# Fourteen late gate groups of a hybrid linear-attention block: plain products replaced by Strassen block products over pairs of groups and pairs of token tiles

## The chip, the cores and the metric

The kernel runs on one core of one Trainium2 chip. The metric is the device time of one execution in microseconds (us). Engines are called as the profile calls them: PE (TensorE matmul), PEld (its weight loads), DVE (VectorE), ACT (ScalarE), POOL (GpSimd) and SP (SyncE, which issues the DMAs here).

## The reference, cut to what matters

One adaLN-modulated layer over 2048 latent tokens with a context prefix of 256 tokens, model width 1024, all in float32. A modulated RMSNorm gives `h`; one wide projection of `h` feeds everything else, among it the output gates of two linear-attention mixers (GLA and Gated DeltaNet) and the 2048 columns of merge gates:

```
z = jnp.matmul(h, w_in).astype(f32)
aq, ak, av, ag, alr, bq, bk, bv, bg, bbeta, bdec, mg = split_cols(z)
...
gates = jax.nn.sigmoid(mg + b_gate.astype(jnp.float32))
merged = gates[..., :D_MODEL] * jnp.matmul(ya, w_gla_out) + gates[..., D_MODEL:] * jnp.matmul(yb, w_gdn_out)
return jnp.matmul(merged, w_o)
```

The change touches only how a part of `mg` (14 of its 16 groups of 128 columns) is computed from `h` and `w_in`.

## The kernel before, in words

The work is four stages one behind the other: a front (modulation vector, RMSNorm, transposes), a projection stage, the chunk-wise preparation of Gated DeltaNet ("gdn"), and then the scans ("mix") and the output stage. PE runs its instructions in the order in which they stand in its queue, and so do DVE, ACT, POOL and SP; a scheduler of the tile framework writes these five queues when the kernel is built, from the order of the program, from its own model of readiness, and from when buffers come free.

**The operands.** `h` is kept in SBUF transposed and split in two: `hi` (the value rounded to the matmul's fp32r format) and `lo` (the rest). The latent tokens are four tiles of 512, each tile with 8 slices of 128 rows of `h` (KD = 8). A weight group of 128 columns of `w_in` is loaded raw (512 KB, `raw_w`), split by ACT into `wh` and by POOL into `wl` (`split_w`). A product of one group with one tile (`tile_mm`, L371) is 8 x 3 = 24 matmuls of 128x128 by 128x512: hi by hi, hi by lo, lo by hi, summed in one PSUM buffer `pz` of three. `gate_eat` (L420) then makes the tanh on ACT and SP writes the tile to `d_gate` in DRAM.

**Where the gates stand.** Groups 8 and 9 are made in the front, groups 0 to 7 in the projection stage (`slots`, one group after the other over all four tiles), and the other fourteen, 10 to 23, are the *late* groups: `gates_dense` is a generator over 14 groups x 4 tiles x 4 steps of 6 matmuls = 224 steps. `phase_proj` weaves it with the gdn preparation: 18 chunks of 128 tokens and one step more, each with its share `int(total * (i + 1) / (NCH + 1.25))` of the steps, so 224/19.25 = 11.6 steps to a chunk.

**The gdn preparation.** `gdn_front(c)` makes the masks and key products of chunk c: POOL multiplies the log-decays by a mask (`R`, L914, four a chunk), PE sums them (L920, L921), ACT takes the exp (L923), POOL multiplies (`n`, L917 and L924; `dec`, L926), PE forms the key products (L936), DVE multiplies them in (L940), ACT and POOL split `n` into `nhi` and `nlo` (L945, L946). `gdn_solve(d, c)` inverts a triangular matrix for both directions by doubling: PE (L988), ACT (L989), PE (L995, L996), DVE (L873), six times over, then POOL's `rt` (L1001), DVE (L1006), and three more products. Front of chunk c and solve of chunk c-1 stand in the same weave.

## Time and profile before

| | us |
|---|---|
| median of 3 runs (lowest, highest) | 2163.72 (2163.07, 2163.72) |
| profiled execution, time | 2161.12 |
| its span, first to last instruction | 2159.3 |
| busy: PE, DVE, ACT, POOL | 2062.3, 1215.5, 899.0, 858.6 |
| last tanh of an early gate, start | 828.86 |
| last tanh of a late gate, start | 1362.9 |

A "row" of the page or of a view has the source line, the engine, the operation, output and input tiles, shapes, the count after an x, then busy time and the mean duration of one in ns; behind the second bar stands how long the engine sat idle just before these instructions, and what ended the wait. The window rows give, for a stretch of the execution, its length, the busy time of each engine with the number of instructions, the granted PE clock (1.00 is full), the share of the DMA engines and GB/s. A matmul's duration is longer than its spacing to the next, since matmuls are pipelined: the pace is read from start to start.

### The profile page before, as it was taken

What the parts mean: (1) busy time and instruction counts of PE and PEld (TensorE: products, weight loads), DVE (VectorE), ACT (ScalarE), POOL (GpSimd) and SP (SyncE); (2) the same over time, 40 slices, a digit from 0 to 9 for tenths busy, and PEclk for the clock granted to TensorE, in tenths of its full rate; (3) what the DMA queues carried; (4) which work ended last, traced back from release to release, by engine and by line L of the source; (5) the groups of instructions that cost most, each with busy time, mean ns of one, the idle gap of its engine ahead of it and who ended that gap; (6) DMA issues with size and microseconds to landing.
All of it is one profiled execution on the core that took longest, in us unless ns stands there. A gap on an engine that the chain in (4) does not pass through costs nothing.

```text
span 2159.3 us, 41811 instructions
## 1 busy us (share of the span) xinstructions
PE 2062.3 (96%) x16096; PEld 1730.3 (80%) x16096; DVE 1215.5 (56%) x2185; ACT 899.0 (42%) x2212; POOL 858.6 (40%) x779
## 2 busy tenths in 40 slices
PE   5999999999999999999999999899988888999998
PEld 2688888888888888777777777788888777999888
DVE  3813555556777553556555555566677776444333
ACT  4644255555452223443434443355555554112111
POOL 2410122222221015666666663456566664222331
PEclk9999999999999999999999999999999999999999
DMA  8323122222222224444434344778888868333222
GB/s 288 104 86 116 50 69 64 63 62 72 61 62 80 71 80 133 138 138 152 143 127 148 128 142 140 262 286 292 308 281 288 285 212 273 130 134 114 98 88 79
DMA packets 275012, 315.60 MB, mean 146 GB/s; under 512 B 22280, under 2 KB 206844, under 8 KB 274812
## 3 DMA queue, kind: packets, MB, share of 16 engines
q1 hardware_dynamic: 274812, 312.92, 43.9%
q8 instruction: 127, 2.08, 0.4%
q14 instruction: 73, 0.60, 0.1%
HBM read 203.00 MB, written 109.84 MB: 145 GB/s over the span
## 4 chain that ended last, share of the span: by engine, by line
PE 82%; DVE 5%; ACT 5%; DMA 3%; POOL 2%; issue 2%; SPq 1%; DVEq 0%; POOLq 0%; ACTq 0%
PE pz L371 46%; PE pz L1661 8%; PE pm L1592 8%; DMA g<-dg 2%; PE pe L936 1%; PE pe L1118 1%; PE pl L995 1%; PE pl L988 1%; PE pl L996 1%; PE pz L1080 1%; DVE ql L1215 1%; ACT E L1209 1%; PE pz L1059 1%; PE pq L614 1%; PE pz L1347 1%
## 5 line engine op out<-in xcount | busy, mean ns | idle before, releaser
L371 PE MATMUL pz<-hi,wh 128*128 128x512 f32 (+1 forms) x1560 | 621.6, 399 | 1.5 <-DVE hi L134 1.5
L371 PE MATMUL pz<-lo,wh 128*128 128x512 f32 (+1 forms) x1560 | 600.3, 385 | 1.8 <-POOL lo L135 1.8
L371 PE MATMUL pz<-hi,wl 128*128 128x512 f32 (+1 forms) x1520 | 588.4, 387 | 0.0
L371 PEld LDWEIGHTS pz<-lo,wh 128*128 128x128 f32 x1560 | 294.7, 189 | 51.0 <-POOL lo L135 3.6
L371 PEld LDWEIGHTS pz<-hi,wh 128*128 128x128 f32 x1560 | 294.3, 189 | 47.8 <-DVE hi L134 2.4
L371 PEld LDWEIGHTS pz<-hi,wl 128*128 128x128 f32 x1520 | 286.1, 188 | 53.9 <-issue 0.4
L135 POOL TENSOR_TENSOR wl<-w,wh 128x1024 fp32r<-128x1024 f32 x44 | 110.0, 2500 | 437.5 <-ACT wh L132 312.0
L569 DVE SCALAR_TENSOR_TENSOR acc<-zpad,cw,acc 128x1024 f32<-128x1024 f32 x192 | 272.3, 1418 | 6.6
L1592 PE MATMUL pm<-yh,wab 128*128 128x256 f32 x1024 | 188.2, 285 | 2.2 <-ACT fsq L1402 1.4
L873 DVE CAST_PREDICATED U<-kit,pl 128x256 f16<-128x256 int32 x216 | 91.1, 431 | 139.2 <-PE pl L996 135.4
L1592 PEld LDWEIGHTS pm<-yh,wab 128*128 128x128 f32 x1024 | 161.8, 193 | 3.1 <-ACT fsq L1402 1.6
L1661 PE MATMUL pz<-wo,mh 128*128 128x512 f32 (+1 forms) x528 | 161.3, 388 | 0.0
L1592 PE MATMUL pm<-yl,wab 128*128 128x256 f32 x512 | 145.5, 284 | 0.0
L989 ACT CAST ppb<-pl 128x256 f16<-128x256 f32 x216 | 73.5, 373 | 166.7 <-PE pl L988 160.3
L1216 POOL TENSOR_TENSOR E<-E,ak 128x256 f32<-128x256 f32 x96 | 78.9, 841 | 110.6 <-ACT E L1209 67.0
L1661 PEld LDWEIGHTS pz<-wo,mh 128*128 128x128 f32 x528 | 98.2, 189 | 20.1
L135 DVE TENSOR_TENSOR sql<-sq,sqh 128x512 fp32r<-128x512 f32 (+1 forms) x36 | 28.0, 804 | 140.5 <-ACT sqh L132 140.2
L624 POOL TENSOR_TENSOR acc<-acc,sq 128x512 f32<-128x512 f32 x32 | 50.6, 1586 | 137.7 <-ACT sq L623 77.7
L1661 PE MATMUL pz<-wo,ml 128*128 128x512 f32 (+1 forms) x264 | 102.0, 386 | 0.0
L1592 PEld LDWEIGHTS pm<-yl,wab 128*128 128x128 f32 x512 | 98.9, 193 | 0.3
L135 POOL TENSOR_TENSOR yl<-wr,yh 128x1024 fp32r<-128x1024 f32 x16 | 39.2, 2462 | 128.2 <-ACT yh L132 128.2
L1666 DVE TENSOR_TENSOR mt<-pz,gtb 128x512 f32<-128x512 f32 (+1 forms) x33 | 22.3, 675 | 115.3 <-PE pz L1661 113.1
(299 smaller groups left out, 4117.5 us busy)
## 6 DMA issues: line engine op xcount, KB each, us to landing
dgate<-ob SPq DMA_DIRECT2D x96, 256.0 KB, 2.1
gd<-dgd SPq DMA_DIRECT2D x32, 768.0 KB, 7.5
w<-in_w_in SPq DMA_DIRECT2D x44, 512.0 KB, 3.6
qk<-dqkv SPq DMA_DIRECT2D x32, 512.0 KB, 6.0
ga<-dgate SPq DMA_DIRECT2D x64, 256.0 KB, 2.8
dqkv<-acc SPq DMA_DIRECT2D x192, 64.0 KB, 1.6
dgd<-tm SPq DMA_DIRECT2D x36, 256.0 KB, 2.9
dgd<-n SPq DMA_DIRECT2D x36, 256.0 KB, 3.4
```

Source lines behind the costliest of these rows:

```text
L135: getattr(nc, lo).tensor_tensor(dst_lo, src, dst_hi.bitcast(F32), op=ALU.subtract)
L371: nc.tensor.matmul(ps[:, 0:n], a[:, kk, :], b[:, kk, :], start=(k == 0), stop=(k == last - 1))
L569: nc.vector.scalar_tensor_tensor(acc, src, wcol, acc, op0=ALU.mult, op1=ALU.add)
L614: nc.tensor.matmul(u[4][:, 0:u[2]], self.ones, u[3][i], start=(i == 0), stop=(i == 1))
L624: nc.gpsimd.tensor_tensor(v, v, r, op=ALU.mult)
L873: self.nc.vector.copy_predicated(out, mv, data)
L936: nc.tensor.matmul(ps[:, o + a * P:o + 256], qk[:, 1, h, :], kq[:, h, a:2, :], start=True, stop=True)
L989: nc.scalar.copy(ppl, pc.rearrange("p h (j i) -> p h j i", i=m))
L1216: nc.gpsimd.tensor_tensor(E[:, :, li, 1], E[:, :, li, 1], k, op=ALU.mult)
L1592: nc.tensor.matmul(ps[:, half * 256:half * 256 + 256], wab[wi][:, k, j * P:(j + 1) * P], yy[:, k, :], start=(i == 0), stop=(i == 11))
L1661: nc.tensor.matmul(ps, aa[:, k, i * P:(i + 1) * P], wo[k][wi][:, cs], start=(j == 0), stop=(j == 23))
L1666: nc.vector.tensor_tensor(sq, ps, gtb[:, cs], op=ALU.mult)
```

## The change

The late groups are taken two by two (7 pairs), and the token tiles two by two (0 with 1, 2 with 3), 14 units in all. In a unit the two weight groups, cut in two halves of the 1024 rows, are a 2x2 block matrix A, and the two token tiles, cut the same way, a 2x2 block matrix B. Winograd's form of Strassen's product needs seven block products instead of eight:

- sums of weights: S1 = A21+A22, S2 = S1-A11, S3 = A22-S2, S4 = A12-S2, made by DVE (`w_sums`) for every unit, and the hi/lo split of the seven left factors (`w_halves`: ACT, and POOL for five, DVE for two);
- sums of tokens: T1 = B12-B11, T3 = B22-B12, T2 = T1-form plus B22, T4 = B21-T2, made once for each pair of tiles, split again into hi and lo, and put in place of tiles that are no longer needed. For that the front writes every slice of `h` to DRAM (`d_h`, 32 DMAs of 256 KB), and `h_first`, `h_fourth` and `h_next` read it back;
- each product is 4 x 3 = 12 matmuls (L558 of the changed kernel, "DENSE" for short below); seven products are 84 matmuls where the plain form had 96. The fourteen units are 1176 matmuls instead of 1344, in 196 steps of 6 instead of 224;
- three PSUM buffers a unit (`a`, `c`, `b`) are summed over several products; between them ACT copies intermediate sums to SBUF (four a unit), DVE adds two, POOL one, and ACT makes the same four tanh as before.

The pair (0, 1) needs T1, T2, T3, T4 when the late gates begin: `h_first` and `h_fourth` hang on the last early gate group, whose tiles are taken in the order 2, 3, 1, 0; T1 to T3 are built in place of tiles 2 and 3 behind its second tile, T4 behind its third. The pair (2, 3) is built during the seventh unit (`h_next`). The weights of the first pair are loaded into a pool that lies where the buffers of `h_first` lay. Pools `wz` and `zs` move to the other side of SBUF.

```diff
+PRODUCTS = (("A11", "B11"), ("S1", "T1"), ("S2", "T2"), ("A12", "B21"), ("S3", "T3"), ("S4", "B22"), ("A22", "T4"))
...
         x2ctx = ExitStack()
         hx2 = self.pool("hx2", 4, ctx=x2ctx)
         hc = self.pool("hTc", 1, ctx=actx, side="right")
+        self.wz = self.pool("wz", 2, ctx=actx, side="right")
+        self.zs = self.pool("zs", 2, ctx=actx, side="right")
         tiles = [(2 + 4 * i, 4, 0) for i in range(4)] + [(0, 2, 1)]
         self.hT = [None] * 5
 
...
+            b, ks = k2 // 2, slice(2 * (k2 % 2), 2 * (k2 % 2) + 2)
+            self.split(hi[b][:, ks, ws], lo[b][:, ks, ws], ht, hi="vector", lo="vector" if k2 % 2 else "gpsimd")
+            if ti < 4:
+                nc.sync.dma_start(self.d_h[ti][b][:, ks, ws], ht)
             yield
...
-                nc.tensor.matmul(ps[:, 0:n], a[:, kk, :], b[:, kk, :], start=(k == 0), stop=(k == last - 1))
+                nc.tensor.matmul(ps[:, 0:n], a[:, kk, :], b[kk // 4][:, kk % 4, :], start=(k == 0), stop=(k == last - 1))
...
-    def gates_dense(self, groups, w):
...
-                yield from self.tile_mm(w, self.hT[ti], self.gate_eat(g), 6)
-                if ti == 1 and raw is not None:
-                    nw = self.split_w(raw)
+    def halves(self, hi, lo, raw, eng):
+        self.nc.scalar.copy(hi, raw.bitcast(F32))
+        eng.tensor_tensor(lo, raw.bitcast(F32), hi.bitcast(F32), op=ALU.subtract)
+
+    def h_raw(self, dst, i, k):
+        self.nc.sync.dma_start(dst.bitcast(F32), self.d_h[i][k])
+
+    def h_sum(self, dst, a, b, op):
+        self.nc.vector.tensor_tensor(dst, a.bitcast(F32), b.bitcast(F32), op=op)
+
+    def h_split(self, blk):
+        self.halves(*blk, blk[1], self.nc.gpsimd)
...
+    def h_t123(self, pieces, t1, t2, t3):
+        for k in range(KD // 2):
+            b11, b12, b22, x, y = pieces(k)
+            self.h_sum(y, b22, b12, ALU.subtract)
+            self.h_sum(x, b12, b11, ALU.subtract)
+            self.halves(t1[0][:, k], t1[1][:, k], x, self.nc.gpsimd)
+            self.halves(t3[0][:, k], t3[1][:, k], y, self.nc.vector)
+            self.h_sum(y, y, b11, ALU.add)
+            self.halves(t2[0][:, k], t2[1][:, k], y, self.nc.gpsimd)
+
+    def h_t4(self, t4, t2, i):
+        for k in range(KD // 2):
+            x = self.hr.tile([P, 512], F32, name=f"r{k % 2}")
+            self.nc.sync.dma_start(x, self.d_h[i][1][:, k])
+            self.h_sum(x, x, t2[0][:, k], ALU.subtract)
+            self.h_sum(x, x, t2[1][:, k], ALU.subtract)
+            self.halves(t4[0][:, k], t4[1][:, k], x, (self.nc.gpsimd, self.nc.vector)[k % 2])
+
+    def h_first(self):
+        b = self.hb8 = [(self.hT[i][2][k], self.hT[i][3][k]) for i in range(4) for k in range(2)]
+        self.hctx.close()
+        self.hr = self.pool("hr", 2, ctx=self.hctx)
+
+        def pieces(k):
+            r = [self.hr.tile([P, 512], F32, name=f"r{j}") for j in range(3)]
+            for t, (i, h) in zip(r, ((0, 0), (1, 0), (1, 1))):
+                self.nc.sync.dma_start(t, self.d_h[i][h][:, k])
+            return *r, r[1], r[2]
+        self.h_t123(pieces, b[4], b[6], b[5])
+
+    def h_fourth(self):
+        b = self.hb8
+        self.h_t4(b[2], b[6], 0)
+        self.hb = {"B11": b[0], "B21": b[1], "T2": b[6], "T1": b[4], "T3": b[5], "B22": b[3], "T4": b[2]}
+
+    def h_next(self, p, i):
+        o = [self.hb[r] for _, r in PRODUCTS]
+        if p == 0:
+            self.h_raw(o[0][1], i, 0)
+            self.h_raw(o[0][0], i + 1, 0)
+        elif p == 1:
+            self.h_raw(o[1][1], i + 1, 1)
+        elif p == 4:
+            raws = o[0][1], o[0][0], o[1][1]
+            self.h_t123(lambda k: (*[t[:, k] for t in raws], *[self.hr.tile([P, 512], F32, name=f"r{j}") for j in range(2)]),
+                        o[2], o[4], o[3])
...
+        elif p == 5:
+            self.h_raw(o[5][1], i, 1)
+            self.h_split(o[5])
+        elif p == 6:
+            self.h_split(o[1])
+            self.h_t4(o[6], o[4], i)
+            self.hb = {"B11": o[0], "B22": o[1], "T1": o[2], "T3": o[3], "T2": o[4], "B21": o[5], "T4": o[6]}
+
+    def w_raws(self, pair):
+        wv = self.io["w_in"].rearrange("o (k p) n -> p (o k) n", p=P)
+        w = {}
+        for i, g in enumerate(pair):
...
+            for j in range(2):
+                nm = f"A{i + 1}{j + 1}"
...
+
+    def w_sum(self, w, nm, a, b, op):
+        w[nm] = self.ws.tile([P, KD // 2, P], F32, name="r0" if nm in ("S1", "S3") else "r1", bufs=1) if nm != "S4" else w[b]
+        self.nc.vector.tensor_tensor(w[nm], w[a], w[b], op=op)
...
+    def w_sums(self, w, part):
+        if part == 0:
+            self.w_sum(w, "S1", "A21", "A22", ALU.add)
+            self.w_sum(w, "S2", "S1", "A11", ALU.subtract)
+        else:
+            self.w_sum(w, "S3", "A22", "S2", ALU.subtract)
+            self.w_sum(w, "S4", "A12", "S2", ALU.subtract)
+
+    def w_halves(self, w, p):
+        nm = PRODUCTS[p][0]
+        tile_ = lambda n, b: self.ws.tile([P, KD // 2, P], F32R, name=n, bufs=b)
+        hi, lo, raw = tile_("hi", 4), tile_("lo", 4), w[nm]
+        self.halves(hi, lo, raw, self.nc.vector if nm in ("S1", "S4") else self.nc.gpsimd)
+        w[p] = (hi, lo)
...
+    def gate_fin(self, ob, src, g, ti):
+        nc = self.nc
+        nc.scalar.activation(ob, src, AF.Tanh, bias=self.pc[:, 48 + g - 8:49 + g - 8], scale=0.5)
+        b0 = 2 * ti
...
+
+    def gates_dense(self, pairs):
+        nc = self.nc
+        work = [(pr, ti) for ti in (0, 2) for pr in pairs]
+        tile_ = lambda: self.zs.tile([P, 512], F32, name="ob")
+        w = self.w_raws(pairs[0])
+        self.w_sums(w, 0)
...
+        self.w_sums(w, 1)
+        for i, ((g0, g1), ti) in enumerate(work):
+            nw = self.w_raws(work[i + 1][0]) if i + 1 < len(work) else None
+            for p, (_, r) in enumerate(PRODUCTS):
+                if p == 0:
+                    a = ps = self.pv()
+                elif p == 1:
...
+                    b = ps = self.pv()
...
+                k = 0
...
+                    for x, y in ((0, 0), (0, 1), (1, 0)):
+                        nc.tensor.matmul(ps, w[p][x][:, kk, :], self.hb[r][y][:, kk, :],
+                                         start=(k == 0 and p in (0, 1, 3)), stop=(k == 11), skip_group_check=True)
+                        k += 1
+                        if k == 6:
+                            yield
+                if p in (0, 1, 2, 4):
+                    s = tile_()
+                    nc.scalar.copy(s, ps)
+                if p == 0:
...
+                    s5 = s
+                elif p == 2:
...
+                elif p == 5:
+                    nc.vector.tensor_tensor(s2, c, s2, op=ALU.add)
+                    self.gate_fin(s2, s2, g0, ti + 1)
+                else:
+                    s = tile_()
+                    self.gate_fin(s, a, g1, ti)
+                if p < 4:
+                    self.w_halves(w, p + 3)
+                elif nw is not None:
+                    self.w_halves(nw, p - 4)
+                if nw is not None and p in (3, 6):
+                    self.w_sums(nw, 0 if p == 3 else 1)
...
-    def slots(self, slots, raw, after, w=None):
+    def slots(self, slots, raw, after, w=None, last=None):
...
+            if last and i + 1 == len(slots):
+                tiles = [self.hT[j] for j in last]
...
+            self.d_h = [[dp.tile([P, KD // 2, 512], F32, name=f"dh{i}_{k}") for k in range(2)] for i in range(4)]
...
-            w = self.slots(seq, None, self.gate_cols(late[0]), w)
+            hooks = seq[-1][3]
+            hooks.setdefault(1, []).append(self.h_first)
+            hooks.setdefault(2, []).append(self.h_fourth)
+            self.slots(seq, None, None, w, last=(2, 3, 1, 0))
...
+            self.hctx.close()
+            self.ws = self.pool("ws", 2, ctx=ctx)
+            self.zs = self.pool("zs2", 4, ctx=ctx)
...
-            dense = self.gates_dense(late, w)
-            total = len(late) * 4 * 4
+            pairs = list(zip(late[0::2], late[1::2]))
+            dense = self.gates_dense(pairs)
+            total = len(pairs) * 2 * 14
```

Three places show how the queues move. **PE, where the late gates begin**, before. L371 are the matmuls of a group with a tile (here the first late group, which follows the last early one without a break), L920 and L921 the sums of log-decays of gdn:

```order
L371 MATMUL pz<-hi_214,wl 128x512
L371 MATMUL pz<-hi_214,wh 128x512
L371 MATMUL pz<-lo_215,wh 128x512
L371 MATMUL pz<-hi_214,wl 128x512
L920 MATMUL pe<-R,m_6471 128x512
L921 MATMUL pe<-R,m_6471 128x512
L371 MATMUL pz<-hi_214,wh 128x512
L371 MATMUL pz<-lo_215,wh 128x512
L371 MATMUL pz<-hi_214,wl 128x512
```

The same place in the changed kernel, where L375 are the last matmuls of the last early group, L1091 and L1092 stand for L920 and L921, L1107, L1123 and L1131 are the key products of the gdn front (L936, L952 and L960 before) and L1150 a transposition that uses `nhi` (L979 before):

```order
L375 MATMUL pz<-hi_1_223,wh 128x512
L375 MATMUL pz<-lo_1_225,wh 128x512
L375 MATMUL pz<-hi_1_223,wl 128x512
L1091 MATMUL pe<-R,m_6612 128x512
L1092 MATMUL pe<-R,m_6612 128x512
L1091 MATMUL pe<-R,m_6612 128x512
L1092 MATMUL pe<-R,m_6612 128x512
L1107 MATMUL pe<-gqk 128x128 x4
L1123 MATMUL pe<-kf,gqk 128x128 x4
L1131 MATMUL pe<-kf,gv 128x128 x4
L1150 LDWEIGHTS nhi
L1150 MATMUL pl<-id_6613,nhi 128x64
```

Where late matmuls stood, gdn work of the first chunk now follows, and the first late matmul (L558) comes 29 rows below the last one shown, behind the first solve steps (L1159, L988 before).

**POOL at the same place**, before. L914, L917 and L924 are the products of the gdn front, `wl` is the weight split, `nlo` the split of `n`:

```order
L914 TENSOR_TENSOR R<-ghi,kf 128x512
L914 TENSOR_TENSOR R<-glo,kf 128x512
L917 TENSOR_TENSOR n_6509<-negb,kf 128x512
L917 TENSOR_TENSOR n_6533<-negb,kf 128x512
L917 TENSOR_TENSOR n_6677<-negb,kf 128x512
L135 TENSOR_TENSOR wl<-w,wh 128x1024
L914 TENSOR_TENSOR R<-ghi,kf 128x512
L914 TENSOR_TENSOR R<-glo,kf 128x512
L924 TENSOR_TENSOR n_6509<-n_6509,dec 128x512
L914 TENSOR_TENSOR R<-ghi,kf 128x512
L914 TENSOR_TENSOR R<-glo,kf 128x512
```

In the changed kernel `lo_...<-r_...` are splits of token sums (T1 to T4 of the first pair of tiles), `lo<-A...` and `lo<-r...` with plain `hi` splits of left factors (A11 and S2), L1085, L1088, L1095 and L1117 the former L914, L917, L924 and L946:

```order
L432 TENSOR_TENSOR lo_0_232<-r_6492,hi_0_230 128x512
L432 TENSOR_TENSOR lo_0_918<-r_6493,hi_0_916 128x512
L432 TENSOR_TENSOR lo_0_228<-r_6535,hi_0_226 128x512
L432 TENSOR_TENSOR lo_0_228<-r_6547,hi_0_226 128x512
L1117 TENSOR_TENSOR nlo<-n_6644,nhi 128x512
L1117 TENSOR_TENSOR nlo<-n_6710,nhi 128x512
L1088 TENSOR_TENSOR n_6944<-negb,kf 128x512
L1085 TENSOR_TENSOR R<-ghi,kf 128x512
L1085 TENSOR_TENSOR R<-glo,kf 128x512
L432 TENSOR_TENSOR lo<-A_6646,hi 128x512
L1095 TENSOR_TENSOR n_6867<-n_6867,dec 128x512
L432 TENSOR_TENSOR lo<-r_6656,hi 128x512
```

A11's split, which the first block product reads, is the tenth of these rows. From the first split of a token sum to this row POOL has 27 rows, eleven of them splits of 128x512; before, one `wl` of 128x1024 stood among the same products of gdn.

**POOL where the seventh unit hands over to the eighth**, in the changed kernel: the last splits of T1 and T2 of the second pair of tiles (`r_...`), of B22, B11 and B21 (128x2048), of a left factor, and between them the former L914 to L926, L946 and L1001 (L1085 to L1097, L1117, L1172):

```order
L1097 TENSOR_TENSOR dec<-dec,kf 128x512
L1073 TENSOR_TENSOR R<-R 128x256
L432 TENSOR_TENSOR lo_0_918<-r_10778,hi_0_916 128x512
L432 TENSOR_TENSOR lo_1_233<-r_10768,hi_1_231 128x512
L432 TENSOR_TENSOR lo<-r_10663,hi 128x512
L432 TENSOR_TENSOR lo_0_232<-lo_0_232,hi_0_230 128x2048
L432 TENSOR_TENSOR lo_0_224<-lo_0_224,hi_0_222 128x2048
L432 TENSOR_TENSOR lo_1_229<-lo_1_229,hi_1_227 128x2048
L432 TENSOR_TENSOR lo_1_233<-r_10779,hi_1_231 128x512
L1117 TENSOR_TENSOR nlo<-n_10703,nhi 128x512
L432 TENSOR_TENSOR lo<-A_10309,hi 128x512
L1172 TENSOR_TENSOR rt<-id_6613,U 128x512 x2
```

In a chunk of the kernel before, the same stretch of the gdn work holds one late split:

```order
L924 TENSOR_TENSOR n_7166<-n_7166,dec 128x512
L926 TENSOR_TENSOR dec<-dec,kf 128x512
L914 TENSOR_TENSOR R<-ghi,kf 128x512
L924 TENSOR_TENSOR n_7237<-n_7237,dec 128x512
L926 TENSOR_TENSOR dec<-dec,kf 128x512
L902 TENSOR_TENSOR R<-R 128x256
L946 TENSOR_TENSOR nlo<-n_7166,nhi 128x512
L1001 TENSOR_TENSOR rt<-id_6472,U 128x512 x2
L946 TENSOR_TENSOR nlo<-n_7237,nhi 128x512
L135 TENSOR_TENSOR wl<-w,wh 128x1024
L917 TENSOR_TENSOR n_7611<-negb,kf 128x512
```

Three splits of 128x2048 and the splits of the token sums stand ahead of that chunk's `nlo` and `rt`, where one `wl` of 128x1024 stood.

51 lines of the change are left out of this document (36 added, 15 removed).

## Prediction

> **What bounds the kernel now.** I read the page first, then the windows over the stretch in which the late gates are made, then the chain of waits inside that stretch. The page's chain by engine, and its first lines by source line:
>
> ```profile
> PE 82%; DVE 5%; ACT 5%; DMA 3%; POOL 2%; issue 2%; SPq 1%; DVEq 0%; POOLq 0%; ACTq 0%
> PE pz L371 46%; PE pz L1661 8%; PE pm L1592 8%; DMA g<-dg 2%; PE pe L936 1%; PE pe L1118 1%; PE pl L995 1%; PE pl L988 1%; PE pl L996 1%; PE pz L1080 1%; DVE ql L1215 1%; ACT E L1209 1%; PE pz L1059 1%; PE pq L614 1%; PE pz L1347 1%
> ```
>
> Nearly half of the span is L371, of which the late gates are a part. The windows (length, then busy time of PE, PEld, DVE, ACT and POOL, then granted clock, DMA share, GB/s), first over the start of the late gates and then over the body of the stage:
>
> ```profile
> 815.00:830.00 15.00, 15.00 (x68) 12.43 (x67) 7.27 (x13) 3.28 (x5) 7.46 (x8) 1.00 0.48 150
> 830.00:845.00 15.00, 15.00 (x75) 12.50 (x74) 4.54 (x9) 4.93 (x8) 11.63 (x10) 1.00 0.48 143
> 830.00:1330.00 500.00, 497.17 (x4901) 386.84 (x4900) 281.54 (x727) 205.03 (x458) 312.58 (x270) 1.00 0.42 137
> ```
>
> PE is busy 497.17 of 500 us; POOL, 312.58, comes second. The stage (828.86 to 1362.9 in the table above, 534 us) is PE's, and at its start PE has no gap at all. So every matmul taken out here shortens the kernel by its spacing, and every stretch in which PE finds no matmul ready lengthens it by its full length. The change does both.
>
> **What it removes.** Pieces of the chain, in order of time (start, length, what):
>
> ```profile
> 1086.20 1.46 PE pz L371 x6
> ...
> 1089.86 0.31 PE pe L920
> 1090.17 0.24 PE pe L921
> ...
> 1092.39 0.86 PE pe L936 x4
> 1093.25 0.23 PE pl L988 x8
> 1093.48 1.45 PE pz L371 x6
> ...
> 1098.16 0.44 PE pe L952 x4
> ...
> 1101.42 0.45 PE pe L960 x4
> ```
>
> A step of six late matmuls costs 1.46 us on the chain. It was 224 steps and becomes 196: 28 x 1.46 = **-41 us**. Between two tiles of the last early group, which nothing interrupts, the spacing is
>
> ```profile
> 817.21 0.60 ACT L417 ACTIVATE ob<-pz 128x512 f32<-128x512 f32 x1 [2.47 <-PE pz L371]
> 822.64 0.60 ACT L417 ACTIVATE ob<-pz 128x512 f32<-128x512 f32 x1 [4.84 <-PE pz L371]
> ```
>
> 5.43 us for 24 matmuls, 0.226 each; by that pace 168 matmuls are 38 us, the lower bound of the gain. I take 41, since the chain's pieces stand in the stage itself. The work of gdn on PE is the same as before.
>
> **What it adds on POOL, and the hole at the start.** POOL in this stage, by groups (count, busy us, mean ns), then two splits of 128x512 from the groups of the whole run, and an addition:
>
> ```profile
> L924 POOL TENSOR_TENSOR n<-n,dec 128x512 f32<-128x512 f32 x36 | 46.3, 1285 | 2.8 <-DVE U L873 2.6
> L946 POOL TENSOR_TENSOR nlo<-n,nhi 128x512 f16<-128x512 f32 x36 | 42.3, 1176 | 44.1 <-ACT nhi L945 44.1
> L926 POOL TENSOR_TENSOR dec<-dec,kf 128x512 f32<-128x512 f32 x32 | 41.2, 1286 | 2.4
> L1001 POOL TENSOR_TENSOR rt<-id,U 128x512 f16<-128x512 f16 x36 | 41.0, 1160 | 36.3 <-ACT U L880 36.3
> L914 POOL TENSOR_TENSOR R<-glo,kf 128x512 fp32r<-128x512 f32 x35 | 36.6, 1045 | 55.5 <-PE pe L905 51.3 <-DMA dgd<-n 4.1
> L914 POOL TENSOR_TENSOR R<-ghi,kf 128x512 fp32r<-128x512 f32 x35 | 36.4, 1041 | 55.0 <-PE pe L920 35.3 <-PE pe L921 19.7
> L917 POOL TENSOR_TENSOR n<-negb,kf 128x512 f32<-128x512 f32 x33 | 34.5, 1044 | 9.0 <-DMA dgd<-n 5.0 <-ACT ppb L989 3.0
> L135 POOL TENSOR_TENSOR wl<-w,wh 128x1024 fp32r<-128x1024 f32 x13 | 31.2, 2397 | 9.9 <-ACT wh L132 9.8
> L902 POOL TENSOR_TENSOR R<-R 128x256 f32<-128x256 f32 x16 | 11.8, 737 | 1.7 <-DMA R<-daqk 1.7
> ```
>
> ```profile
> L135 POOL TENSOR_TENSOR lo<-hf,hi 128x512 fp32r<-128x512 f32 x18 | 25.8, 1433 | 35.2 <-DVE hi L134 35.2
> L135 POOL TENSOR_TENSOR gl<-g,gh 128x512 fp32r<-128x512 f32 x16 | 20.4, 1275 | 15.2 <-ACT gh L132 15.2
> ```
>
> and, from the page,
>
> ```profile
> L624 POOL TENSOR_TENSOR acc<-acc,sq 128x512 f32<-128x512 f32 x32 | 50.6, 1586 | 137.7 <-ACT sq L623 77.7
> ```
>
> A split of 128x512 (`lo`) is not in this stage before. Its bounds are 1.275 (`gl`, same shape and types, beside a quiet DVE) and 1.433 (`lo` of the front, beside a busy one); I take 1.28, since `gl` and L924 of the stage itself agree.
>
> The first block product reads A11's `lo`. POOL takes its rows in order, and from the first split of a token sum to A11's stand 27 rows (the order above shows the last of them): eleven splits (11 x 1.28 = 14.1), eight R (8.4), four n (4.2), two n by dec (2.6), two nlo (2.4), 31.6 us in all. They can't begin much before the end of the early gates, E, about 828: the tiles that T1 to T3 overwrite are in use until the second tile of the last early group is done, 10.9 us before E (2 x 5.43). Then SP issues the reads, and each sum needs three pieces of 256 KB. Rows of the DMA issues (KB each, us to landing):
>
> ```profile
> gd<-dgd SPq DMA_DIRECT2D x32, 768.0 KB, 7.5
> ...
> ga<-dgate SPq DMA_DIRECT2D x64, 256.0 KB, 2.8
> ```
>
> For three pieces together I take 5 us, between one transfer of 256 KB (2.8) and one of 768 (7.5), then the sum on DVE, the cast on ACT and two waits, so that POOL starts its first split some 2 us before E. A11's split is then done at about E + 30. Of the eight R, those beyond the buffers wait for PE's sums anyway, which stand behind the last early matmul. Meanwhile PE has only what its order shows ahead of the first L558: two pairs like L920 with L921 (1.1 us), L936, L952, L960 (1.75) and some 14 small ones like L988 (8 in 0.23): 3.3 us. That leaves a hole of 26 to 27, and with a reload of the two-deep buffers that the T pieces rotate through, **+28 us**. Ends: 23, if the splits run closer together, 33, if they run at 1.433 and T4's pieces come late. Who waits: everything on PE, since it takes its rows in order; what covered this place before was the first late group's own matmuls.
>
> **The hole at the turn.** Between the seventh and eighth unit the second pair of tiles is built. Its sums may be written only when the seventh unit's fifth product has read T3. From there to B11's split, which the eighth unit's first product reads, POOL has ten splits of 128x512 (12.8), two of 128x2048 (B22 ahead of B11; each twice `wl`'s 2.397, 9.6), four R, two n, two n by dec, two dec, one R of 128x256 and the unit's own addition (13.5): 35.9 us. PE has in that time two products (24 matmuls, 5.9) and the gdn pieces that its order holds there, about 12.5 by the chain's lengths: 18.4. **+17 us** (35.9 - 18.4 = 17.5; ends 10, if a part of the splits finds POOL ahead, and 24, if contention lengthens them as in the `lo` row). What hid such a wait before was late matmuls; here the late matmuls are the ones that wait.
>
> **The rest, in small terms.** At a unit's start `a` takes the PSUM buffer of the previous `a`, whose tanh (ACT, 0.69) starts only when the seventh product is done; other gdn work of 0.25 to 1.3 us lies between. 13 boundaries x 0.2: +3 (0 to 9). On ACT, DVE and POOL each unit brings four copies (0.6), seven casts and eight DVE operations
>
> ```profile
> L1006 DVE TENSOR_TENSOR rt<-pl,rt 128x512 f16<-128x512 f32 x36 | 23.8, 688 | 28.6 <-PE pl L1005 25.2 <-POOL rt L1001 3.3
> ```
>
> of 0.69; the doubling of gdn's triangular solve passes through these queues six times a chunk, and a piece behind a 0.69 us operation is late by up to that. PE has late matmuls in between to cover it, fewer than before: +4 (0 to 15). The 32 writes of `d_h` (8 MB) stand on SP among the front's loads: +1 (0 to 3), with no gain possible. The clock, in the front:
>
> ```profile
> 50.00:55.00 5.00, 2.71 (x10) 1.27 (x10) 3.82 (x8) 4.58 (x12) 1.96 (x2) 0.69 0.46 165
> 55.00:60.00 5.00, 4.35 (x12) 3.08 (x13) 3.58 (x7) 1.97 (x5) 2.34 (x2) 0.50 0.68 259
> ```
>
> After a stretch in which PE was busy 2.71 of 5 us the next 5 us were granted 0.50. Two long holes, each with up to one such half-rate stretch behind it, lose 2.5 us at most apiece: I take +2 (0 to 5). [...]
>
> **The sum.** -41 + 28 + 17 + 3 + 4 + 2 + 1 = **+14 us**. On the profiled execution's 2161.12 that is 2175; the median of the runs lies 2.6 above the profiled one, so **2178**. A measurement of this kernel can tell about 0.2%, 4.3 us: 2159.4 to 2168.0 counts as no change.
>
> **Rivals.**
>
> *The holes are short (faster).* POOL's R and n products of the first chunk stand between the splits, but might have run before E while the token pieces were still coming in. Then only the splits and two nlo remain (16.5), and the start costs 17; at the turn the lower end, 10; the rest 6. -41 + 33 = -8: 2156. For it: POOL is busy only 7.46 of 15 us ahead of 830. Against: the order is fixed, and the first R rows stand behind the first splits. It decides when holes and waits together cost less than 37. Chance 0.16.
>
> *Holes and saving cancel (no change).* 23 + 12 + 6 = 41: 2164. Chance 0.16; nothing favours it but that it lies between.
>
> *POOL becomes the bound (slower still).* A chunk has 290 us / 18 = 16.1 us of gdn work on POOL (the nine groups less `wl`). Per unit come five splits and one addition, 7.7 us, 14 x 7.7 / 18 = 6.0: 22.1 of the 25.6 that a chunk will last ((534 - 41) / 19.25). That fits by 14%. But `acc` (L624) takes 1.586 where L924 with the same shape takes 1.285, beside a DVE that is busy with long operations of two inputs. With that factor, 1.23, it is 27.3 a chunk, and 18 x 1.7 = 30 us more: 2208. It decides where the mean split exceeds 1.48 us. [...] Against: DVE's extra per chunk is only 14 x 8 x 0.69 / 18 = 4.3 us, so it lies beside POOL's work a fraction of the time. Chance 0.11.
>
> That the change doesn't do what it says can be left out: PE's order holds 1176 late matmuls for 1344.
>
> **How the numbers follow.** My forecast (holes and waits of 45 to 81 us, 2168 to 2204) has 0.57, the likeliest single value 2178. Slower: 0.57 + 0.11 = 0.68; same 0.16; faster 0.16. The range, 2152 to 2204, takes in the faster rival but for a tail of 0.06, and leaves out of the slower side about 0.10.
>
> **What would show it.** Right: in the profile after, an idle stretch of PE of 23 to 33 us behind about 828, with POOL busy all through it and the first L558 waiting for POOL's `lo`; a second one of 10 to 24 us in the middle of the stage, ended by POOL's 128x2048 split; a granted clock below 1.00 just behind both; the group of L558 with 1176 matmuls; otherwise PE busy as before, and chunks of about 25.6 us. Wrong: no idle stretch at 828 longer than 15 us, or PE idle spread over all chunks and POOL's splits over 1.48 us (then POOL is the bound), or the end of the stage less than 41 us earlier than the holes explain.

## The result, and the profile after

| | before | after |
|---|---|---|
| median of 4 runs, us | 2163.51 | 2321.74 |
| lowest, highest | 2163.07, 2163.72 | 2317.85, 2322.47 |
| ratio, with 95% interval | | 1.0728 (1.0709 to 1.0747) |
| span of the profiled execution | 2159.3 | 2319.6 |

The changed kernel is 158 us slower. The forecast was 2178 with a range to 2204: the sign held, the size did not, and most of the loss came from what the sum had priced at 4 us or had left out.

Where it went is read from the windows of the changed kernel (columns as in the prediction): the end of the early gates, the start of the late ones, the chunks up to the turn, the turn, and the chunks behind it.

```profile
800.00:850.00 50.00, 50.00 (x227) 40.78 (x227) 26.45 (x33) 11.72 (x16) 3.58 (x3) 1.00 0.29 89
850.00:892.00 42.00, 12.41 (x49) 7.97 (x47) 36.52 (x40) 14.45 (x24) 34.28 (x26) 0.55 0.41 118
892.00:1150.00 258.00, 230.87 (x2126) 172.72 (x2126) 174.01 (x367) 123.31 (x265) 174.43 (x148) 0.94 0.44 135
1150.00:1290.00 140.00, 107.85 (x890) 77.91 (x889) 118.11 (x188) 65.00 (x128) 107.99 (x75) 0.84 0.43 137
1290.00:1520.00 230.00, 207.02 (x1994) 154.25 (x1993) 158.02 (x347) 109.06 (x240) 148.39 (x124) 0.96 0.43 134
```

Before, PE was busy 497 of 500 us at a clock of 1.00. Now the start (second row) and the turn (fourth) stand out, as forecast. But in the third and fifth rows, with no token sums in them, PE is idle for a tenth of the time and the granted clock is 0.94 and 0.96. Those 488 us were expected to run as before.

The early gates, which the change hardly touches, end 24 us late: their last matmul starts at 851.9, before at 827.7. Of these, 9.3 us are there by the 200th of the 3,296 early matmuls (126.1 for 116.8), when their pace can have cost 1 us. The front moves more bytes and PE runs longer at half rate in it (20.5 us between 48 and 80, before 10.2 us). The same 50 us there, before and then after:

```profile
60.00:110.00 50.00, 48.78 (x247) 36.13 (x246) 39.64 (x67) 33.84 (x64) 23.45 (x19) 0.98 0.25 78
```

```profile
60.00:110.00 50.00, 47.48 (x223) 35.03 (x223) 35.45 (x63) 30.71 (x59) 21.38 (x18) 0.91 0.73 233
```

No run takes the writes of the tokens out of the front, so how much of the 9 us is theirs, and how much the halved token tiles', stays open. The other 15 us come after that, bit by bit. Four starts in a row of plain matmuls, before and then after:

```profile
820.18 0.39 PE L371 MATMUL pz<-hi,wl 128*128 128x512 f32 x1
820.41 0.39 PE L371 MATMUL pz<-hi,wh 128*128 128x512 f32 x1
820.63 0.39 PE L371 MATMUL pz<-lo,wh 128*128 128x512 f32 x1
820.86 0.39 PE L371 MATMUL pz<-hi,wl 128*128 128x512 f32 x1
```

```profile
820.21 0.40 PE L375 MATMUL pz<-lo,wh 128*128 128x512 f32 x1
820.45 0.40 PE L375 MATMUL pz<-hi,wl 128*128 128x512 f32 x1
820.68 0.39 PE L375 MATMUL pz<-hi,wh 128*128 128x512 f32 x1
820.91 0.40 PE L375 MATMUL pz<-lo,wh 128*128 128x512 f32 x1
```

Three steps take 0.68 us before and 0.70 after; the mean over some 830 pairs between 600 and 810 us is 0.2269 and 0.2334 us. PE is busy 209.9 and 210.0 of those 210 us: here the busy share doesn't show the slower pace, only the spacing of the starts does.

What PE waits for from the first late matmul on, and how one such wait comes about (the rows of PE that wait, then ACT's and POOL's around 1090; in the brackets the engine's idle time ahead of the row and what ended it):

```profile
PE pl L1159 <- DVE U L1044: 42.2, 37, 3.4
PE pl L1166 <- ACT ppb L1160: 11.5, 6, 4.5
PE pl L1181 <- DVE rt L1177: 9.1, 15, 0.8
```

```profile
1091.53 0.21 PE L1166 MATMUL pl<-ppb,Tm 128*128 128x64 f16 x1 [4.50 <-ACT ppb L1160]
```

```profile
1083.84 0.58 ACT L565 COPY ob<-pz 128x512 f32<-128x512 f32 x1
1090.50 0.72 ACT L530 ACTIVATE ob<-ob,pc 128x512 f32<-128x512 f32 x1 [6.08 <-POOL ob L576]
1091.13 0.62 ACT L1160 CAST ppb<-pl 128x256 f16<-128x256 f32 x2
```

```profile
1085.52 1.28 POOL L1097 TENSOR_TENSOR dec<-dec,kf 128x512 f32<-128x512 f32 x1
1088.52 0.72 POOL L1073 TENSOR_TENSOR R<-R 128x256 f32<-128x256 f32 x1 [1.72 <-DMA R<-daqk]
1089.20 1.26 POOL L576 TENSOR_TENSOR ob<-ob 128x512 f32<-128x512 f32 x1
```

Read from the bottom: POOL's addition of a unit (L576) stands behind a gdn row that waits for a DMA; ACT's tanh (L530) waits for the addition, and ACT does nothing for 6 us; the small cast `ppb` of gdn's solve, whose input was there since about 1086.5, stands behind that tanh; PE waits 4.5 us for `ppb`. No engine is short of time there. And then the clock: the window of the wait and the two windows behind it.

```profile
1086.20:1091.50 5.30, 0.83 (x11) 0.52 (x10) 1.06 (x3) 1.00 (x3) 2.55 (x3) 0.84 0.24 67
1091.50:1094.90 3.40, 3.37 (x22) 2.91 (x22) 2.73 (x8) 0.25 (x1) 0.00 (x0) 0.50 0.22 77
1094.90:1098.30 3.40, 3.40 (x21) 2.42 (x20) 1.92 (x4) 2.47 (x6) 1.88 (x2) 0.74 0.24 11
```

PE is busy again from 1091.5, but at half rate: the granted clock is 0.50. In this trace two 128x512 matmuls in a row at 0.50 start 0.427 us apart (median of 85 pairs), at 1.00 0.234. Between 891 and 1520 us the trace has 96 us at half rate, some 48 us lost (an estimate: half of it, by the granted 0.50), on top of about 80 us of waits.

### The profile page after: what moved, and what is told of

Same layout as the page of the kernel before. It is cut to its first block, busy times and chain, and to the rows that moved or that the text cites. A ratio compares the mean times of both kernels' runs of the same rounds, so it can differ in the third digit from the quotient of the medians.

```text
span 2319.6 us, 42254 instructions
## 1 busy us (share of the span) xinstructions
PE 2107.5 (91%) x15928; PEld 1733.1 (75%) x15928; DVE 1397.6 (60%) x2349; ACT 994.6 (43%) x2387; POOL 1005.6 (43%) x872
## 5 line engine op out<-in xcount | busy, mean ns | idle before, releaser
L375 PE MATMUL pz<-hi,wh 128*128 128x512 f32 (+1 forms) x1112 | 431.5, 389 | 4.1 <-DVE wh L407 2.1
L375 PE MATMUL pz<-lo,wh 128*128 128x512 f32 (+1 forms) x1112 | 429.6, 387 | 1.6 <-POOL lo L136 1.6
L375 PE MATMUL pz<-hi,wl 128*128 128x512 f32 (+1 forms) x1072 | 413.9, 386 | 0.0
L375 PEld LDWEIGHTS pz<-hi,wh 128*128 128x128 f32 x1112 | 210.1, 189 | 48.7 <-DVE hi L135 2.9
L375 PEld LDWEIGHTS pz<-lo,wh 128*128 128x128 f32 x1112 | 210.4, 189 | 45.9 <-POOL lo L136 3.3
L375 PEld LDWEIGHTS pz<-hi,wl 128*128 128x128 f32 x1072 | 202.5, 189 | 42.9 <-issue 0.4
L558 PE MATMUL pz<-hi,hi 128*128 128x512 f32 x392 | 181.1, 463 | 2.6 <-ACT hi L431 1.4
L558 PE MATMUL pz<-hi,lo 128*128 128x512 f32 x392 | 171.1, 437 | 1.3 <-POOL lo L432 1.3
L558 PE MATMUL pz<-lo,hi 128*128 128x512 f32 x392 | 166.5, 425 | 1.7 <-POOL lo L432 1.7
L1044 DVE CAST_PREDICATED U<-kit,pl 128x256 f16<-128x256 int32 x216 | 92.0, 429 | 78.1 <-PE pl L1167 77.5
L1159 PEld LDWEIGHTS <-nhi 128*128 128x128 f16 x864 | 41.3, 102 | 97.2 <-issue 77.2
```

Of the source, the lines that this page charges most:

```text
L375: nc.tensor.matmul(ps[:, 0:n], a[:, kk, :], b[kk // 4][:, kk % 4, :], start=(k == 0), stop=(k == last - 1))
L558: nc.tensor.matmul(ps, w[p][x][:, kk, :], self.hb[r][y][:, kk, :], start=(k == 0 and p in (0, 1, 3)), stop=(k == 11), skip_group_check=True)
L1044: self.nc.vector.copy_predicated(out, mv, data)
L1159: nc.tensor.matmul(pc[:, h], nhi[:, h], ul[:, h], start=True, stop=True)
```

## The experiments

The theory behind the first eight, called *queues*: the change's operations on DVE, ACT and POOL stand in in-order queues ahead of the small steps of gdn's triangular solve, and PE waits for those. Its rival, *cover*: with an eighth fewer late matmuls PE has too little to bridge the latency of the solve, whatever the queues hold. The runs were made on four chips, on which the kernel before took 2159 to 2167; so each time stands beside the kernel before on the same chip, and what is compared is the distance between the two (158.2 for the changed kernel). Most runs are single ones, good to some 5 us.

**e2_fewer**, the kernel before with the matmuls of one slice in eight left out of the late products:

```diff
-        k, last = 0, len(terms) * KD
-        for kk in range(KD):
+        k, last = 0, len(terms) * nk
+        for kk in range(nk):
...
-                yield from self.tile_mm(w, self.hT[ti], self.gate_eat(g), 6)
+                yield from self.tile_mm(w, self.hT[ti], self.gate_eat(g), 6, KD - 1)
```

> The kernel before with the last of the eight slices left out of every late product: 21 matmuls instead of 24, 1176 in the stage, as many as in the changed kernel, in the same steps and with no other work. It leaves out an eighth of the sum of the late gates. Theory queues (the new operations of the change stand ahead of gdn's chain in the in-order queues of DVE and ACT, and that makes PE wait): PE loses nothing but the matmuls, the stage shortens by 35 to 41 us, 2163 becomes 2122 to 2130. Rival cover (with an eighth fewer late matmuls PE has too little to bridge the latency of gdn's chain): waits of PE on DVE's U appear, half-rate windows with them, and the gain is under 20 us, 2145 or more.

Measured 2140.6 beside 2160.0: 19.4 less, half of what 168 matmuls take. What PE waits for in this kernel's stage, where the kernel before had 3.5 us:

```profile
PE pl L1010 <- DVE rt L1006: 6.0, 4, 1.5
PE pl L988 <- DVE U L873: 4.1, 5, 1.8
PE pl L979 <- ACT n L1019: 1.6, 3, 0.9
```

Here the rival is right: pure removal already uncovers the solve. 12 us of waits and 13.7 us at half rate (3.4 before; half of such time counted as lost, by the granted 0.50) are some 13 of the 19 us that are missing.

**e3_fourteen**, the changed kernel with 14 matmuls in a product:

```diff
-                    for x, y in ((0, 0), (0, 1), (1, 0)):
+                    for x, y in ((0, 0), (0, 1), (1, 0)) + ((0, 0),) * (kk % 2):
```

> The changed kernel with 14 matmuls in each block product instead of 12 (two of them repeated): 1372 late matmuls, 28 more than before the change, all side work as in the changed kernel. It adds terms to the sums that do not belong there. Theory queues: the added 196 matmuls cost 44 us of PE, of which the cover of existing waits gives back a part; PE's waits on DVE and ACT shrink but do not vanish; 2335 to 2360. Rival cover: the waits and most of the half-rate windows vanish, and the time stays or falls, 2280 to 2322.

Measured 2329.5 beside 2160.0, between the two: 196 more matmuls (44 us) raise the distance from 158 to 169.5, by 11 us. But with more late matmuls than the kernel before had, PE still waits:

```profile
PE pl L1159 <- DVE U L1044: 31.6, 29, 3.8
PE pl L1181 <- DVE rt L1177: 7.1, 10, 1.8
PE pl L1166 <- ACT ppb L1160: 5.6, 5, 2.2
```

So cover explains a part, and the side work makes waits that full cover doesn't hide.

**e4_noweights**, no weight work from the second unit on:

```diff
-            nw = self.w_raws(work[i + 1][0]) if i + 1 < len(work) else None
+            nw = None
...
-                if p < 4:
-                    self.w_halves(w, p + 3)
+                if p == 0 and i == 0:
+                    self.w_halves(w, 3)
+                    w.update({q: w[q - 4] for q in (4, 5, 6)})
...
-            w = nw
```

> The changed kernel in which the weights of the first pair stand for all pairs (four left factors, used again for the last three products): the loads, sums and splits of weights of units 2 to 14 are left out, so that these products are wrong; token sums, copies, additions and tanh stay. Theory queues: without four sums and two splits on DVE, seven casts on ACT and five splits on POOL per unit, the chunks outside start and turn lose most of their waits: from about 33 us a chunk to 27 or less, the whole falls by 60 to 100 us, to 2220 to 2260. Rival cover: the chunks stay over 31 us and the whole above 2290.

Measured 2244.3 beside 2160.0, a distance of 84 instead of 158: 74 us less, the largest single piece. The same 200 us of the stage, outside start and turn, in the kernel before, in the changed kernel and in this one:

```profile
900.00:1100.00 200.00, 197.24 (x1958) 153.04 (x1957) 115.68 (x297) 81.96 (x185) 125.18 (x109) 0.99 0.41 136
```

```profile
900.00:1100.00 200.00, 177.10 (x1627) 132.47 (x1626) 130.27 (x278) 94.37 (x205) 128.88 (x110) 0.94 0.42 126
```

```profile
900.00:1100.00 200.00, 195.25 (x1929) 148.55 (x1927) 114.31 (x297) 88.65 (x200) 115.21 (x104) 1.00 0.36 120
```

PE's idle time falls from 23 to 5 us and the clock is full again, with the same block products, copies and additions. DVE's busy time falls by only 16 of 200 us: it was never the bound.

**e12_nosums** asks which part of the weight work it is; only DVE's sums go:

```diff
-        w[nm] = self.ws.tile([P, KD // 2, P], F32, name="r0" if nm in ("S1", "S3") else "r1", bufs=1) if nm != "S4" else w[b]
-        self.nc.vector.tensor_tensor(w[nm], w[a], w[b], op=op)
+        w[nm] = w[a]
```

> The changed kernel without the four sums of weights that DVE makes per unit: a raw block stands in the place of each sum, the casts, splits, loads and everything else stay (the products with sums are wrong). Leaving out all weight work had brought 77 us. If what counts is that these sums stand in DVE's queue, for 59 us of busy time and 22 us of waiting for POOL to give their buffer free, ahead of the U that PE waits for: at least half of the 77, 2262 to 2285. If it is the casts on ACT and the splits: under 20 us, above 2300.

Measured 2276.2 beside 2162.7, a distance of 113.5: 45 of the 74 us are the four sums per unit. In the changed kernel their rows were

```profile
L511 DVE TENSOR_TENSOR r<-A,r 128x512 f32<-128x512 f32 x28 | 30.4, 1087 | 11.7 <-POOL lo L432 11.5
L511 DVE TENSOR_TENSOR r<-A,A 128x512 f32<-128x512 f32 x14 | 16.4, 1175 | 12.5 <-POOL lo L432 10.4 <-DMA gv<-dqkv 1.2 <-DMA A<-in_w_in 0.9
L511 DVE TENSOR_TENSOR r<-r,A 128x512 f32<-128x512 f32 x14 | 12.4, 886 | 0.2
```

0.89 to 1.18 us each, where the prediction had 0.69, and DVE stands still 22 us until POOL's split has read the single buffer that the sum is written to. Behind them in DVE's queue is the `U` that PE waits for, as around 1050 (two rows of DVE, then PE's):

```profile
1050.33 0.69 DVE L511 TENSOR_TENSOR r<-A,r 128x512 f32<-128x512 f32 x1 [3.12 <-POOL lo L432]
1050.94 0.42 DVE L1044 CAST_PREDICATED U<-kit,pl 128x256 f16<-128x256 int32 x1
```

```profile
1051.41 0.28 PE L1159 MATMUL pl<-U,nhi 128*128 128x64 f16 x4 [2.50 <-DVE U L1044]
```

Without the sums PE's wait for `U` is half of the 42.2 us (L1158 and L1043 stand for L1159 and L1044):

```profile
PE pl L1158 <- DVE U L1043: 20.7, 18, 3.7
```

Outside the turn it falls from 19.5 to 7.6 us, at the turn from 22.7 to 13.1. In the changed kernel, while PE waits those 42.2 us, DVE works 14.4 us on rows that the change added (L432, L438, L511) and stands 3.6 us ahead of L511 for POOL; nearly all of the rest is the solve's own rows, what the solve itself takes when nothing covers it. How much of the 45 us is the place in the queue and how much DVE and POOL getting in each other's way (below) is not separated.

**e5_dveadd**, POOL's addition of a unit moved to DVE:

```diff
-                    nc.gpsimd.tensor_tensor(s, s, s5, op=ALU.add)
+                    nc.vector.tensor_tensor(s, s, s5, op=ALU.add)
```

> The changed kernel with the one addition of a unit that POOL makes (after the fifth product) given to DVE like the other two. Theory queues: the three long waits of PE behind ACT's tanh that waits for this addition (2.6, 4.5 and 2.7 us in the changed kernel) go, with the half-rate windows behind them, against 14 more operations of 0.69 us on DVE: 5 to 25 us less, 2297 to 2317. Rival cover: what PE waits for changes, its sum does not: 2317 to 2327.

Measured 2304.6 beside 2159.2, a distance of 145: 13 us less, in the middle of what *queues* gave: the wait shown above was the longest of six of its kind (11.5 us in the row of `ppb`), of which none is left here, and DVE took 14 more operations.

**e7_notokens** and **e13_noturn** price the two holes. The first leaves out all token sums, the second only those of the seventh unit (`h_next` returns at once):

```diff
-        self.h_t123(pieces, b[4], b[6], b[5])
...
-        self.h_t4(b[2], b[6], 0)
...
     def h_next(self, p, i):
+        return
```

> The changed kernel without the token sums: the block products read the split tiles as they are, nothing is read back from the DRAM copy, no T1 to T4 is built, neither at the start nor in the seventh unit (so five of seven products are wrong). The writes of the copy in the front stay. Start and turn in the changed kernel: 39 us from the last early to the first late matmul, of which about 33 go; and at the turn some 38 us over three chunks, with the waits behind them. Both theories: 65 to 80 us less, 2242 to 2257. If the turn's cost is mere work that PE would wait for elsewhere, only the start's 33 go: about 2288.

> The changed kernel without the second pair's token sums: T1 to T4 of the first pair are built at the start as in the changed kernel, and are used again in units 8 to 14, so that these are wrong; the reads, sums and splits of the seventh unit are left out. Leaving out start and turn together had brought 80 us. By the trace the start is 39 us without late matmuls, with some 5 us of gdn work in it: 32 to 36 us; then the turn is the other 44 to 48, 2274 to 2280. If the turn is worth only what was predicted, 17, then 2305.

Measured 2242.0 beside 2159.2 and 2275.0 beside 2162.7, distances of 83 and 112. The start is worth 30 us (112.4 less 82.7) and the turn 46 (158 less 112). The start in the changed kernel has the size that was forecast; PE's only long wait there is for a DVE row, which itself stands behind the token sums.

```profile
862.33 2.11 PE L1107 MATMUL pe<-gqk 128*128 128x128 f32 x8
885.50 1.09 PE L1123 MATMUL pe<-kf,gqk 128*128 128x128 f32 x4 [21.06 <-DVE n L1111]
```

So DVE's queue ended the long wait, and not POOL's as the prediction had it. A11's split on POOL came later still, at 894.0, 42 us behind the last early matmul where the prediction had 30, and PE waited another 1.3 us for it. At the turn the two get in each other's way (DVE's rows, then POOL's):

```profile
1196.64 0.68 DVE L432 TENSOR_TENSOR lo<-r,hi 128x512 fp32r<-128x512 f32 x1
1197.24 0.41 DVE L1044 CAST_PREDICATED U<-kit,pl 128x256 f16<-128x256 int32 x1
1197.57 4.71 DVE L432 TENSOR_TENSOR lo<-r,hi 128x512 fp32r<-128x512 f32 x1
1202.21 0.41 DVE L1044 CAST_PREDICATED Tm<-kit,pl 128x256 f16<-128x256 int32 x1
```

```profile
1196.80 4.94 POOL L432 TENSOR_TENSOR lo<-lo,hi 128x2048 fp32r<-128x2048 f32 x1 [0.63 <-DVE r L438]
```

The same DVE operation takes 0.68 us where it starts ahead of POOL's long split and 4.71 us where it starts while that runs; it ends at 1202.28, 0.54 us after the split (1201.74).

**e8_products**, both cuts (e4 and e7) together:

> The changed kernel without token sums and without the weight work of units 2 to 14 (the two cuts together): seven products, copies, additions and tanh are left, the products are wrong. If all loss beyond the spacing of plain matmuls (22 us) and the copy of the tokens lies in the side work: as the kernel before with an eighth of the late matmuls left out, plus these, 2140 + 25 = 2165, and up to 2180 with the ACT copies. If the block products themselves cost (summing over several products in one buffer, buffers handed from unit to unit): over 2190.

Measured 2177.6 beside 2159.2, a distance of 18, within the first forecast. By the profile none of it lies in the stage (here: from the last early matmul to the last late one, 534.8 us before): that takes 519.3 us, 15.5 less than before, where e2's takes 513.6. So copies, additions and buffers between units cost some 6 us, and the loss stands ahead of the stage (its last early matmul comes 23.5 us late) and behind it (8.5 us, in a part that the change doesn't touch and that took 797 to 804 us in the other runs, 805 here). Its stage holds 3.4 us at half rate, as many as before.

**e9_shift32** turns to the spacing: the kernel before with its split weights moved by 32 bytes.

```diff
+        self.pool("wpad", 1, ctx=ctx).tile([P, 8], F32, name="wpad")
         self.wz = self.pool("wz", 2, ctx=ctx)
         self.zs = self.pool("zs", 2, ctx=ctx)
+        self.pool("zpad", 1, ctx=ctx).tile([P, 24], F32, name="zpad2")
```

> The kernel before with 32 bytes ahead of the pool of split weights and 96 behind it: the weights begin 32 bytes off a multiple of 64, the token tiles stay where they were (three of four) or move by 128 bytes. Nothing else. If the weights' alignment sets the spacing of plain matmuls: 0.233 instead of 0.227 us in the projection stage, and with 3,300 early and 1,344 late products of 0.0066 each up to 31 us more, 2180 to 2192. If it was the place or the halved token tiles: 2160 to 2164, 0.227.

Measured 2179.4 beside 2159.2, with a spacing of 0.2333 us: one pad of 32 bytes costs 20 us (14 of them by the last early matmul), and brings the changed kernel's spacing without its other side of SBUF or its halved token tiles.

**e1_align**, the changed kernel with a pad of 32 bytes that makes the weights' address a multiple of 64:

```diff
+        self.pool("wpad", 1, ctx=actx, side="right").tile([P, 8], F32, name="wpad")
         self.wz = self.pool("wz", 2, ctx=actx, side="right")
```

> The changed kernel with a pad of 32 bytes ahead of the pool of split weights, so that each weight block of 128 columns begins at a multiple of 64 bytes again (in the changed kernel it begins 32 bytes off one). Two explanations for the spacing of plain matmuls that rose from 0.227 to 0.233 us in the projection stage: (a) the alignment of the weights: then the spacing is 0.227 again, the early gates end about 22 us earlier (near 830 instead of 852) and the whole takes about 2300; (b) the place of the weights on the other side of the memory, or the halved token tiles: then spacing and time stay, 0.233 and 2322.

Measured 2307.5 beside 2160.0, a distance of 147.4, 11 us less, spacing 0.229, the last early matmul at 841: better, but neither of the two forecasts. **e14_shift64** and **e15_shift128** therefore set two more offsets in the kernel before (pads of 64 and 64, and of 128 and none, in e9's places):

> The kernel before with the split weights moved by 64 bytes (and 64 behind them, so that three of the four token tiles keep their place and the fourth moves by 128). If alignment to 64 bytes is what counts, the spacing is 0.227 us and the time 2160; if only a multiple of 512, the length of a weight row, runs at full pace, then as with a pad of 32 bytes in the changed kernel some 0.229 to 0.230, 2166 to 2172.

> The kernel before with the split weights moved by 128 bytes (the fourth token tile too). Alignment to 64 or 128 bytes as the rule: 0.227 us, 2160. Offset within 512 bytes as the rule: as with the pad of 96 bytes in the changed kernel some 0.232, 2173 to 2178.

Measured 2180.5 and 2174.9 beside 2166.6: e14 lies above both of its forecasts, e15 in the second. All spacings, by the weights' offset within 512 bytes (the length of one row of a weight block; worked out from the pools, as no view shows an address). With the pads in the kernel before, the fourth token tile lies 128 bytes further, the others where they were:

| offset, bytes | run | mean spacing, us | first three tiles | fourth tile |
|---|---|---|---|---|
| 0 | before | 0.2269 | 0.2270 | 0.2267 |
| 32 | e9 | 0.2333 | 0.2333 | 0.2336 |
| 64 | e14 | 0.2323 | 0.2334 | 0.2290 |
| 128 | e15 | 0.2315 | 0.2327 | 0.2276 |
| 384 | e10 | 0.2324 | alike | alike |
| 448 | e1 | 0.2292 | alike | alike |
| 480 | after | 0.2334 | alike | alike |

Alignment to 64 or 128 bytes is refuted as the rule. It isn't the weights' address alone either: in e15 the fourth tile, moved by 128 bytes like the weights, runs at nearly the old pace, and the tiles that stayed do not. What fits all rows is the distance between weights and tile, if the tiles of the changed kernel lie at offset 0: none gives 0.227 to 0.228, weights 64 bytes below the tile (e14's fourth, e1) 0.229, and every other distance 0.232 to 0.234. No run was made to test that.

**e10_repairs**, the whole of the changed kernel with e5's edit and a pad of 96 bytes:

> The changed kernel, correct, with two repairs: a pad of 96 bytes, so that each weight block begins at a multiple of 128 bytes, and the fifth product's addition on DVE. The two alone brought 14 (with a pad of 32 bytes) and 17 us. If they add up: 2290; if a multiple of 128 bytes brings the full spacing of 0.227 us: 2280. In no case near 2160.

Measured 2298.2 beside 2162.7, above both forecasts, but a distance of 135.5, 23 us less: as the two alone gave here (13 and 11), though with another spacing (0.2324, worse than with the smaller pad).

**e11_ceiling**, e8 with the pad of 96 bytes:

> The changed kernel without token sums and without the weight work of units 2 to 14, as before, and with the pad of 96 bytes: what the seven products would give if all side work but the copies, additions and tanh were free and the plain matmuls as fast as before (the products are wrong). 2178 less 11 to 22 us for the spacing: 2156 to 2167. Theory: no gain is left for the change even then, since the lost cover takes back half of the removed matmuls (20 of 38 us) and the copies the rest. If it comes out under 2145, the change could pay with cheaper side work.

Measured 2172.85 (2169.26 to 2177.86) beside 2162.67, ratio 1.0053 (1.0033 to 1.0074), above the forecast of 2156 to 2167: with all weight and token work for nothing the changed kernel is still slower than the one before, by 10 us. The theory in the forecast, that nothing of the gain is left in the stage, is not borne out: the stage takes 519.6 us, 15.2 less than before. What takes it back stands ahead of it: the last early matmul comes 21.3 us late, 8.4 of them by the 200th, the rest with the spacing. With the old front and spacing it would be some 11 us faster than before (an estimate, 21.3 less 10.2); that wasn't measured.

## Why the prediction was wrong

The sum was -41 + 28 + 17 + 3 + 4 + 2 + 1. Against the runs, by the stages of the profiled executions (667.7 us in the changed kernel, 534.8 before, 513.6 in e2, 588.5 in e4, 590.8 in e7, 519.3 in e8, 621.4 in e13), which leave out what varies from chip to chip elsewhere and so differ by a few us from the distances above:

| term | predicted | measured | from |
|---|---|---|---|
| 28 steps fewer | -41 | -21 | e2 less before |
| start | +28 (23 to 33) | +31 | e13 less e7 |
| turn | +17 (10 to 24) | +46 | after less e13 |
| collisions of the weight work | +4 (0 to 15), with all else | +79 | after less e4 |
| unit boundaries, copies | +3 (0 to 9) | +6 | e8 less e2 |
| clock | +2 (0 to 5) | some 48 us in the stage, held in the rows above | clock rows |
| writes of the tokens | +1 (0 to 3) | +9, with all else in the front | start of the 200th early matmul |
| spacing of early matmuls | none | +15 | from the 200th to the last |

Start, turn and weight work overlap (together they bring 148 us, from after to e8, singly 156), so that 8 go off again; 3 us come behind the last late matmul. That makes the 160 us by which the profiled executions differ.

The step that failed worst is "PE has late matmuls in between to cover it, fewer than before: +4 (0 to 15)"; by e4 it is 74 to 79 us. I compared busy sums: 22.1 of 25.6 us a chunk on POOL, 4.3 us more on DVE, so it fits. It does fit; no engine became the bound, and the rival of POOL as the bound fell with it (POOL was busy 68% in the third window row, and its splits took about 1.37 us, under the 1.48 from which it was to decide; that threshold takes all of POOL's rows as stretched alike, and with the splits alone stretched it is 2.2). What counts for an engine that runs in order is not its sum but what stands and waits in its queue ahead of the step that PE needs next. Each new row that waits (a sum for POOL to free a buffer, a tanh for POOL's addition) holds up the solve's casts behind it. The prediction named such rows only for start and turn.

The second failure is "28 x 1.46 = -41": the price of the removed steps was right, but the steps were also the cover of the solve's latency. The trace of before held a sign of how thin that cover was. One wait of 2.5 us stands there, and the half-rate window behind it:

```profile
1020.46 0.61 PE L988 MATMUL pl<-U,nhi 128*128 128x64 f16 x8 [2.48 <-DVE U L873]
```

```profile
1017.90:1021.30 3.40, 0.88 (x11) 0.67 (x11) 2.85 (x7) 0.52 (x2) 1.34 (x2) 1.00 0.95 252
1021.30:1024.70 3.40, 3.40 (x23) 2.49 (x22) 0.77 (x3) 0.18 (x1) 1.04 (x1) 0.51 0.15 56
```

PE at 497 of 500 us means that nothing was ever late, not that there was room for lateness. This row was the warning: the wait is for `U`, the row that PE waits 42 us for in the changed kernel, and each such wait costs up to 1.7 us more in clock (an estimate: half of the 3.40 us window at 0.51). The third failure is the turn, priced from POOL's sum and PE's work alone: DVE's rows there, held behind POOL's long splits (4.71 us for 0.68), hold up the solve of that chunk and the next. The start was right in size, with luck: DVE, not POOL, held PE for 21 of the 30 us that PE stood idle, and A11's split was 12 us later than priced. The writes of the tokens were priced at 1 us, and the front lost 9, of which no run says how much is theirs. The spacing was in no term: that a pool moves to the other side of SBUF was read as harmless.

## What to carry to other kernels

A kernel that is bound by one engine with a latency chain woven through it has two budgets: that engine's time and the cover of the chain; work that is taken off the bound engine is taken off the cover too, so try the pure removal (e2) before building the replacement. Price an added operation on an off-path engine by what it may wait for and by what stands behind it in that queue, not by its duration. When a pool moves, compare the spacing of matmuls from start to start, since the busy shares hid it here (209.9 and 210.0 of 210 us).

## What the runs showed of the hardware that was not expected

**The clock answers to short idle.** The granted clock changes on a grid of 3.41 us, and only between 1.00 and 0.50 (60 records in the trace of the changed kernel, 20 before). Between the first and the last late matmul of the changed kernel, 17 grid windows at full rate were followed by one at half rate, and in these PE (with its weight loads) had been idle for 1.61 to 2.83 us of the 3.41; in the 137 that were followed by a full one it had been idle for at most 1.68 us. Before, it was one window with 2.52 us against 152 with at most 0.83. In all sixteen traces together, 97 grid windows at full rate were followed by one at half rate, in 96 of them with 1.56 us idle or more; of 2,383 that were followed by a full one, none had more than 1.91 us; between the two values both occur. So here idle time of about half a window sufficed, several short gaps added up (before one half-rate window of the changed kernel 1.61 us, the longest gap 0.95), and a wait of 2 us that brings such a window costs nearly 4 (an estimate: half of 3.41 on top).

**The matmul pace changed with the operands' addresses.** A shift of the stationary operand's block by 32 bytes off a multiple of 512 (e9) lengthened the spacing of 128x128 by 128x512 matmuls from 0.2269 to 0.2333 us (2.8%). Where the moving operand was shifted by 128 bytes along with it (e15, fourth tile), the spacing was 0.2276 us instead of 0.2327. What the rule is stays open.

**Many DVE operations ended only after the POOL operation that was running**: 0.68 us became 4.71 beside a split of 128x2048. In the changed kernel's trace 74 operations of 128x512 with two inputs (L432, L438, L511) start while a POOL operation runs, and every one ends 0.55 us after that one's end, 0.71 to 4.71 us long; the 62 others take 0.68 to 0.69 us. Copies with one input were held too: the 21 of `U<-id` (L1143) that start beside a POOL operation end 0.15 us after it and take 0.79 to 1.38 us, the 15 others 0.28 to 0.30. The `U<-kit,pl` of L1044, with an input from PSUM, were not: the 136 that start beside a POOL operation (one at 1197.24) take 0.41 to 0.46 us, the 80 others 0.41 to 0.45. In the kernel before, the prediction's `gl` did not stand beside a quiet DVE: DVE was busy for 12.4 of the 20.4 us of these 16 splits, and 32 of its 35 operations there read PSUM.
